# A hybrid decoder trunk on one core: the body inside a block that is ordered by the finer of the framework's two timelines

## The chip, the cores and the metric

One core of a Trainium2 chip runs the whole kernel. The metric is device time in microseconds (us) of one execution, as a median over runs. The engines are TensorE (PE, with its weight loader PEld), VectorE (DVE), ScalarE (ACT), GpSimd (POOL) and SyncE (SP), which here only issues transfers. Each engine works through its own queue in order; semaphores tie the queues together.

## The reference

Two layers, each on a stream x of 256 tokens by 1024 channels in float32. A layer normalises x and multiplies it by one wide matrix `w_in` (1024 by 12832). The result feeds three mixers side by side: a Mamba-2 scan (convolution, SiLU, chunked scan with decays), a sliding-window attention with sinks, and an attention with forgetting gates. Each has a SiLU gate and its own projection; the three are merged by sigmoid gates, pass one output projection and are added to x:

```python
for layer in range(DEPTH):
    h = rms_norm(x, norm_w[layer])
    proj = jnp.einsum('bsd,de->bse', h, w_in[layer])
    ...
    y_a = mamba2_branch(...)
    y_b = sliding_window_branch(...)
    y_c = forgetting_attention_branch(...)
    branch = jnp.einsum('bsiw,iwd->bsid', ys, w_proj[layer])
    g = jax.nn.sigmoid(gates.reshape(b, s, N_BRANCH, d) + gate_bias[layer])
    x = x + jnp.einsum('bsd,de->bse', jnp.sum(g * branch, axis=2), w_out[layer])
return rms_norm(x, final_norm_w)
```

## The kernel before, in words

**Precision and pieces.** Every wide product is taken in three passes of a rounded 32-bit type: both factors are split into a high and a low part, and high x high, low x high and high x low are added in PSUM. Weights come in pieces: SP loads a part of 1024 values per partition into one of six `raw` buffers, ScalarE copies it to `hi` (L290) and VectorE subtracts to get `lo` (L291); `hi` and `lo` have six buffers each, and at most four split parts are held ahead of their use (`AHEAD`, in `feed`). TensorE's products are all issued by the helpers `mm` (L109) and `transpose` (L113), so these two lines stand for all of its work.

**The order of TensorE** is written out: a list of operations (`ops`) is walked by `run_op`, and a small planner (`launch`, `pump`, `drain`) slips the short steps of attention and scan between the wide products at due times given by constants such as `D_SOFT` or `D_Q`, counted on an estimate of TensorE's time. These constants say how many microseconds lie between, say, the scores of an attention and the transposes of its probabilities; in that time ScalarE and VectorE must have done the softmax (L610 to L658; the scaling of the windowed one is L639).

**The order of the other engines** is the framework's. It traces all instructions, and when the trace is closed it walks through them on a timing model: whenever an engine of the model is free, it takes the instruction of highest priority (the earliest written, unless raised by `tc.high_priority`) whose inputs the model has ready. Buffers of a pool are given out in the same walk. The order that comes out is then fixed in each engine's queue; on the chip nothing is reordered. The kernel holds this choice by several means: `tc.manual_schedule` keeps the listed engines as written, `pin` (`keep_in_program_order`, L285) ties one instruction behind the one written before it on its engine, and `issue_after` (in `finish`) queues a group behind a given one.

```python
with tc.manual_schedule(engines={ENG.PE, ENG.DVE, ENG.Activation, ENG.Pool}):   # L1425
    ...
with tc.manual_schedule(engines={ENG.PE}):                                      # L1555
    for g in late:
        g()
    for i, f, last in ops[3:]:
        run_op(i, f, last)
```

The first region is the first stage of some 18 us: there the four compute engines are as written, and from then on TensorE alone.

**Lines that the prediction names.** `dma_sum` (L481 to L490) evicts two halves of a product with ScalarE (L486, L487) and lets GpSimd issue a transfer that adds one to the other (L488). The rotated queries and keys are multiplied by VectorE (L551) and combined by GpSimd (L561, L562). L676 ends the transposed probabilities of the windowed attention, L1106 adds a gate's bias while it frees TensorE's bank. L985 is a power on GpSimd with its VectorE reader L989 in `group_norms`; L257 and L259 are the same pair in `row_rsqrt2` at the end of a layer. In `mT` the merged branches are transposed and split again (pinned where marked, so its line is L285). L1205 to L1231 are the end of a layer's output: add, squares, root, scaling, store.

## Time and profile before

| | |
|---|---|
| runs | 806.71, 806.82, 807.55 us (median 806.82) |
| span of the profiled execution | 805.1 us |
| the rest of the median outside that span | 1.7 us |
| instructions in the span | 14840 |
| mean granted TensorE clock | 0.998 |

The span runs from the first to the last instruction of the profiled execution. Its rows give, for each engine, the busy time; for a group of instructions, their number, the mean of one and the idle time of the engine ahead of them with who ended it; and for a wait, how long in all, how many times and the longest. Matmuls overlap in their pipeline, so their mean duration is longer than the distance from one to the next. Idle time of an engine costs something only where TensorE then waits for it.

### The profile page before, as it was taken

The page shows a single profiled execution, that of the slowest core. Times are in us where ns is not written, and L with a number is a line of the kernel's source. Part 1 is how long each engine was busy: PE and PEld are TensorE (multiplying, and loading weights), DVE is VectorE, ACT ScalarE, POOL GpSimd, SP SyncE. Part 2 cuts the span into 40 slices and gives each one's busy share as a digit, 9 for nine tenths or more (in the row PEclk, how much of TensorE's full clock was granted, in tenths as well). Part 3 has the DMA queues.
Part 4 walks back from the last instruction along what each step waited for, and adds up shares of the span by engine and source line. Part 5 has one row for each costly group of instructions (what it writes and reads, how often), then busy time and mean ns, then how long its engine had stood idle before and what let it go on. Part 6 is the DMA issues. An engine that isn't in the chain of part 4 may idle for free.

```text
span 805.1 us, 14840 instructions
## 1 busy us (share of the span) xinstructions
PE 796.5 (99%) x5160; PEld 711.6 (88%) x5160; DVE 684.2 (85%) x1416; ACT 533.8 (66%) x1146; POOL 167.5 (21%) x236
## 2 busy tenths in 40 slices
PE   9999999999999999999999999999999999999996
PEld 8998988888998988888998899888889989888896
DVE  6878999997998997795785799999889999969865
ACT  7776768875775885543665678687657768755452
POOL 3166213140210100033001741122311220002000
PEclk9999999999999999999999999999999999999999
DMA  9997987797765565686678987679976546576632
GB/s 316 280 259 172 253 219 200 219 290 220 198 184 167 174 187 170 219 253 205 217 251 257 239 210 217 157 217 287 285 211 196 183 143 202 156 248 210 209 106 78
DMA packets 138827, 170.43 MB, mean 212 GB/s; under 512 B 9353, under 2 KB 106465, under 8 KB 138753
## 3 DMA queue, kind: packets, MB, share of 16 engines
q1 hardware_dynamic: 114960, 140.53, 55.5%
q0 software_dynamic: 13328, 13.29, 10.3%
q10 hardware_dynamic: 10464, 15.67, 6.7%
q8 instruction: 41, 0.67, 0.3%
q14 instruction: 34, 0.27, 0.1%
HBM read 154.71 MB, written 2.16 MB: 195 GB/s over the span
## 4 chain that ended last, share of the span: by engine, by line
PE 91%; issue 3%; DMA 2%; POOL 2%; DVE 1%; ACT 1%; POOLq 0%; DVEq 0%
PE mm L109 78%; PE mx L109 9%; PE mx L113 4%; DMA L<-L 1%; DMA hb<-in_sinks_dram 1%; POOL L L488 1%; DMA L<-in_x_dram 0%; DVE L L551 0%; ACT pp L610 0%; POOL L L285 0%; POOL L L562 0%; DVE lo L291 0%; POOL sm L224 0%; POOL L L571 0%; POOL L L572 0%
## 5 line engine op out<-in xcount | busy, mean ns | idle before, releaser
L109 PE MATMUL mm<-L,hi 128*128 128x512 f32 x1056 | 354.7, 387 | 0.5 <-ACT L L487 0.3
L291 DVE TENSOR_TENSOR lo<-raw,hi 128x1024 fp32r<-128x1024 f32 (+1 forms) x276 | 313.3, 1154 | 40.9 <-ACT hi L290 36.1
L109 PE MATMUL mm<-hi,L 128*128 128x512 f32 (+2 forms) x1168 | 303.1, 349 | 0.1
L290 ACT ACTIVATE hi<-raw 128x1024 fp32r<-128x1024 f32 (+1 forms) x276 | 265.6, 982 | 50.6 <-PE mm L109 30.0
L109 PE MATMUL mm<-L,lo 128*128 128x256 f32 x1056 | 266.6, 273 | 0.0
L109 PEld LDWEIGHTS mm<-hi,L 128*128 128x128 f32 x1168 | 205.8, 190 | 23.2 <-issue 1.5
L109 PEld LDWEIGHTS mm<-L,hi 128*128 128x128 f32 x1056 | 195.1, 190 | 27.4 <-issue 3.0
L109 PEld LDWEIGHTS mm<-L,lo 128*128 128x128 f32 x1056 | 202.1, 191 | 5.3
L109 PE MATMUL mm<-lo,L 128*128 128x512 f32 (+2 forms) x584 | 201.5, 347 | 0.0
L109 PEld LDWEIGHTS mm<-lo,L 128*128 128x128 f32 x584 | 110.2, 190 | 10.7
L488 POOL DMA_DIRECT2D L<-L x68 | 60.7, 915 | 192.5 <-ACT L L487 155.2
L1074 POOL TENSOR_SCALAR_AFFINE_SELECT bias<-bias 128x128 f32<-128x128 f32 x64 | 30.8, 513 | 82.7 <-DMA bias<-cumd 82.7
L829 DVE SCALAR_TENSOR_TENSOR L<-L,vec,L 128x255 f32<-128x255 f32 (+2 forms) x96 | 46.2, 481 | 1.9 <-ACT L L826 0.4
L486 ACT ACTIVATE L<-mm 128x256 f32<-128x256 f32 x84 | 31.9, 380 | 20.0 <-PE mm L109 14.0
L652 ACT ACTIVATE pp<-pp,nm 128x128 f32<-128x128 f32 x64 | 28.2, 443 | 22.8 <-DVE nm L646 22.8
L1109 ACT ACTIVATE L<-L 128x512 f32<-128x512 f32 x24 | 15.1, 631 | 34.5 <-DVE L L1106 30.8
L610 ACT ACTIVATE pp<-pp,nm 128x128 f32<-128x128 f32 x32 | 12.6, 394 | 24.9 <-DVE nm L615 24.1
L488 POOL DMA_DIRECT2D qt<-L x16 | 14.2, 925 | 71.4 <-ACT qt L487 64.6
L1142 POOL TENSOR_TENSOR L<-L,L 128x512 f32<-128x512 f32 x8 | 12.0, 1494 | 74.0 <-DVE L L1141 74.0
L487 ACT ACTIVATE L<-mm 128x256 f32<-128x256 f32 x68 | 26.2, 386 | 1.5 <-DMA L<-L 1.5
L1106 DVE TENSOR_TENSOR L<-mm,L 128x512 f32<-128x512 f32 x22 | 15.1, 687 | 11.2 <-PE mm L109 11.2
L551 DVE TENSOR_TENSOR L<-L,cs 128x256 f32<-128x256 f32 x40 | 20.0, 536 | 4.6 <-DMA L<-L 4.6
(213 smaller groups left out, 913.7 us busy)
## 6 DMA issues: line engine op xcount, KB each, us to landing
raw<-in_w_in_dram SPq DMA_DIRECT2D x191, 512.0 KB, 5.1
raw<-in_w_proj_dram SPq DMA_DIRECT2D x48, 512.0 KB, 6.0
L<-L POOLq DMA_DIRECT2D x72, 128.0 KB, 5.4
raw<-in_w_out_dram SPq DMA_DIRECT2D x16, 512.0 KB, 5.9
bias<-cumd ACTq DMA_DIRECT2D x16, 256.0 KB, 3.4
L<-cumd ACTq DMA_DIRECT2D x8, 512.0 KB, 5.4
L<-in_gate_bias_dram ACTq DMA_DIRECT2D x12, 256.0 KB, 5.4
qt<-L POOLq DMA_DIRECT2D x16, 128.0 KB, 6.0
```

What stands on the lines that cost most here:

```text
L109: nc.tensor.matmul(o, a, b, **kw)
L113: nc.tensor.transpose(o, a, i)
L290: keep(act)(hi, src, AF.Copy)
L291: keep(tt)(lo, src, hi.bitcast(F32), op=ALU.subtract)
L486: act(halves(lo), ordered(p[:, S:2 * S]), AF.Copy)
L487: last = act(halves(out), ordered(p[:, 0:S]), AF.Copy)
L488: nc.gpsimd.dma_start(out, lo, accum_op=ALU.add)
L551: tt(m, p, cs[:, i, :], op=ALU.mult)
L652: act(pp[:, i, sl], pp[:, i, sl], AF.Exp, scale=-1.0, bias=nm[:, e:e + 1], accum_out=sums[:, e:e + 1])
L829: stt(a[:, s:S], x_[:, 0:S - s], y.vec[:, 16 * j + u:16 * j + u + 1], a[:, s:S], op0=ALU.mult, op1=ALU.add)
L1074: nc.gpsimd.affine_select(out=bias[:, i, dst], in_=bias[:, i, src], compare_op=ALU.is_ge, fill=NEG, base=0, pattern=[[-1, P]], channel_mul ...
L1106: tt(halves(g), p, halves(y.gb), op=ALU.add)
```

## The change

One line is added in `hybrid_trunk`, ahead of the first instruction of the body; the pools are opened before it:

```diff
+    ctx.enter_context(tc.block(schedule_with_timeline_sim=True))
     nw8 = T("L1", [NK, P])
     nc.scalar.dma_start(nw8, norm_w[0:1, :].rearrange("o (k p) -> (o k) p", p=P))
     tab = T("tab", [P, 1])
```

`tc.block` traces what follows into a block of its own that is ordered as a unit: what is traced outside it is not mixed in. With the argument, the walk over the block's instructions runs on the finer of the framework's two timing models; without it, and in the kernel before, it runs on the coarser one. By the framework's own words the coarser one leaves out a fixed cost of GpSimd's elementwise instructions. No operation, tile, buffer count, pin or written order differs.

## The prediction

> **What bounds the kernel now.** I read the page's first lines, then a table of busy time by stage, then the list of who waits for whom on each engine, then the timeline at the places where TensorE starts just after its input. In the group rows below the number after the bar is the busy sum, then the mean of one in ns, then the idle time just before it and who ended it.

> ```profile
> span 805.1 us, 14840 instructions
> ...
> PE 796.5 (99%) x5160; PEld 711.6 (88%) x5160; DVE 684.2 (85%) x1416; ACT 533.8 (66%) x1146; POOL 167.5 (21%) x236
> ...
> L109 PEld LDWEIGHTS mm<-hi,L 128*128 128x128 f32 x1168 | 205.8, 190 | 23.2 <-issue 1.5
> L109 PEld LDWEIGHTS mm<-L,hi 128*128 128x128 f32 x1056 | 195.1, 190 | 27.4 <-issue 3.0
> ```

> The span is 805.1 us and the median of the runs 806.82, so 1.7 us lie outside the span; I add them to every sum. TensorE (PE) is busy 99% of it. A busy share can hide short gaps, so the next view matters more: the busy time of every engine in eight stages (start:end, length, then PE, weight loader, VectorE, ScalarE, GpSimd with their counts, granted clock, DMA share).

> ```profile
> 0.00:18.00 18.00, 16.20 (x112) 15.20 (x113) 12.27 (x27) 13.26 (x27) 5.40 (x20) 1.00 0.93 309
> 18.00:75.00 57.00, 56.87 (x377) 51.74 (x375) 45.29 (x80) 40.46 (x94) 26.37 (x35) 1.00 0.97 255
> 75.00:150.00 75.00, 74.78 (x559) 67.32 (x560) 72.34 (x189) 58.25 (x159) 18.71 (x24) 1.00 0.76 204
> 150.00:300.00 150.00, 149.87 (x1032) 133.38 (x1031) 137.76 (x320) 108.37 (x243) 25.37 (x42) 1.00 0.73 211
> 300.00:387.00 87.00, 87.00 (x435) 76.04 (x434) 65.50 (x80) 43.20 (x55) 16.78 (x18) 1.00 0.64 199
> 387.00:480.00 93.00, 93.00 (x596) 85.13 (x596) 70.92 (x124) 60.51 (x128) 29.00 (x35) 1.00 0.86 242
> 480.00:780.00 300.00, 299.93 (x1939) 265.63 (x1937) 264.48 (x566) 200.55 (x428) 45.87 (x64) 1.00 0.70 206
> 780.00:805.00 25.00, 18.83 (x122) 17.20 (x120) 15.67 (x36) 9.22 (x18) 0.00 (x0) 0.95 0.18 64
> ```

> Between 18 and 780 us PE is idle 0.13 + 0.22 + 0.13 + 0 + 0 + 0.07 = 0.55 us out of 762. The other idle time is 1.80 us ahead of 18 us and 6.17 us in the last stage, most of it after the last product. The granted clock is 1.00 wherever PE works steadily. So **TensorE's own stream is the whole time**: nothing that another engine does can shorten it by more than those crumbs. The list of PE's waits says the same; it has two entries (who waited for whom: total, times, longest):

> ```profile
> PE mx L113 <- POOL ident masks.py:199: 1.5, 1, 1.5
> PE mm L109 <- ACT L L487: 0.3, 1, 0.3
> ```

> The first is the identity matrix at the start, the second one eviction at 75 us.

> **The change part by part.** It adds one line: the body is traced inside a block that the framework orders by its finer timeline of the engines, where it used the coarser one before. No operation is added or removed: 5160 products, 1416 VectorE, 1146 ScalarE and 236 GpSimd instructions and every transfer stay. Three parts have to be priced.

> *TensorE's order* cannot move: from its first product to its last it stands in regions that keep it as written (L1425 and L1555). Price 0.

> *The first 18 us* (to the end of the first region) are written out by hand on the four compute engines, so only the SP queue's transfers could move there. They stand in one queue in program order, x and the first pieces of w_in ahead. Price 0; what could be won back there is at most the 1.80 us of PE idle of that stage.

> *The order on VectorE, ScalarE, GpSimd and of the transfers after that* is what moves. Each of these queues is in order, so an instruction that is put ahead of another delays everything behind it, and one that is put in front while its input is late holds its whole engine. Two things cover this. First, the weight pieces are split well ahead: ScalarE's split waits for PE to give a buffer back, and seldom the other way round.

> ```profile
> ACT hi L290 <- PE mm L109: 30.0, 43, 5.4
> ...
> DVE sm L989 <- POOL sm L985: 3.6, 2, 1.8
> DVE sm L259 <- POOL sm L257: 1.2, 2, 0.8
> ```

> ScalarE waits 43 times, 30.0 us in all, for buffers that PE still reads: the store of split pieces is full at those times, and one late split costs nothing. Second, the written order of PE leaves some microseconds between a step and its use. What a finer timeline could gain is in the other two rows: VectorE stands 3.6 + 1.2 = 4.8 us behind GpSimd's powers. That is VectorE's time, not PE's, so it is worth 0 here.

> The transfers move with their queues (in the rows: count, size, median us from issue to landing):

> ```profile
> raw<-in_w_in_dram SPq DMA_DIRECT2D x191, 512.0 KB, 5.1
> ...
> L<-L POOLq DMA_DIRECT2D x72, 128.0 KB, 5.4
> ```

> SP issues little but weight loads, one as each of six buffers comes free, so their order among themselves has no reason to change; GpSimd's adding transfers are issued behind ScalarE's evictions as now. I cost both at 0; the cover is the six buffers and the three evictions that stand between such a transfer and its reader. Without it one late transfer costs up to its 5.4 us, which is less than the upper bound below.

> The cover is thin at some places, and these carry my sum. In the timeline rows the first number is the start, the second the length; I pair the producer with PE's start behind it.

> ```profile
> 75.19 0.48 PE L109 MATMUL mm<-L,hi 128*128 128x512 f32 x1 [0.31 <-ACT L L487]
> ...
> 123.21 0.69 DVE L639 TENSOR_TENSOR pp<-pp,rsum 128x512 f32<-128x512 f32 x1
> ...
> 124.05 0.63 PE L113 MATMUL mx<-ident,pp 128*128 128x128 f32 x4
> ...
> 150.04 0.69 DVE L1106 TENSOR_TENSOR L<-mm,L 128x512 f32<-128x512 f32 x1
> ...
> 150.84 0.19 PEld L109 LDWEIGHTS mm<-L,hi 128*128 128x128 f32 x1 [0.40 <-issue]
> ...
> 159.78 0.69 DVE L676 TENSOR_TENSOR L<-mx,L 128x512 f32<-128x512 f32 x1
> ...
> 160.69 0.39 PE L109 MATMUL mm<-L,bias 128*64 128x256 f32 x2
> ...
> 386.06 0.69 DVE L285 SCALAR_TENSOR_TENSOR L<-mx,L 128x512 fp32r<-128x512 f32 x1 [0.90 <-ACT L L285]
> ...
> 386.80 0.19 PEld L109 LDWEIGHTS mm<-hi,L 128*128 128x128 f32 x1 [0.15 <-DVE L L285]
> ...
> 518.12 0.69 DVE L639 TENSOR_TENSOR pp<-pp,rsum 128x512 f32<-128x512 f32 x1
> ...
> 518.96 0.63 PE L113 MATMUL mx<-ident,pp 128*128 128x128 f32 x4
> ...
> 780.88 0.69 DVE L285 SCALAR_TENSOR_TENSOR L<-mx,L 128x512 fp32r<-128x512 f32 x1 [0.90 <-ACT L L285]
> ...
> 781.62 0.19 PEld L109 LDWEIGHTS mm<-hi,L 128*128 128x128 f32 x1 [0.16 <-DVE L L285]
> ```

> At 124.05 PE starts 0.15 us after the softmax scaling has ended (123.21 + 0.69 = 123.90); at 150.84 0.11 us after an add that frees its bank; at 160.69 0.22 us after a subtraction; at 386.80 and 781.62 0.05 us after a low half of `merged`. The second layer repeats the first 394.91 us later (518.96 - 124.05), so the middle three count twice: 3 x 2 + 75.19 + 386.80 + 781.62 makes **nine places** with at most 0.22 us to spare.

> The common filler that a new order can put ahead there is one split:

> ```profile
> L291 DVE TENSOR_TENSOR lo<-raw,hi 128x1024 fp32r<-128x1024 f32 x224 | 274.9, 1239 | 29.2 <-ACT hi L290 24.6 <-DMA raw<-in_w_proj_dram 1.6 <-PE mm L109 1.6
> ```

> It takes 1.24 us, so a place that gets one ahead costs 1.24 - 0.15 = 1.1 us. How many places are hit the trace cannot tell. Bounds: none (0) or all nine with two splits each, 9 x (2.48 - 0.15) = 21.0 us. I take five of nine with one split, 5.5 us: about half, because the rule of choice (highest priority among what is ready) stays and only the moments move, and because the two places on `merged` are partly pinned. Other steps have more room, and I cost them at nothing; their cover is the full store and PE's written distances. If that goes, the price is the fourth rival's.

> *The block's borders.* Everything but the pools lies inside, so no work can be cut off by it. The trace does not show such a border; the nearest rows are the entry into the body:

> ```profile
> 0.41 0.10 POOL L1581 MEMSET const-uint8-127<- 128x1 uint8 x1
> 0.81 0.20 POOL masks.py:197 MEMSET ident<- 128x128 f32 x1 [0.29 <-POOLq L1581]
> ```

> GpSimd passes from the preamble into the body in 0.4 us. Two borders: 0 to 0.8 us. I take 0.4. A gain I exclude, as a border only adds.

> Sum on the profiled execution: 805.1 + 5.5 + 0.4 = 811.0, and with 1.7 outside **812.7 us**.

> **The rivals.**

> *No difference (0.18).* The new order differs, but nowhere where PE has no room, or it differs little. For it: 0.55 us of PE idle in 762, and a full store of splits. Against it: nine places with at most 0.22 us. Time 805.2 to 808.4, most likely 807.2 with the borders. That the change does nothing at all (the pins and the written regions leave no freedom) belongs here too.

> *Faster (0.06).* The finer timeline frees VectorE of its waits for GpSimd and thereby the thin places. All that PE can win is 0.55 us in the middle and 1.80 in the first stage: 806.8 - 2.35 = 804.5. It decides only if more than 1.6 of these 2.35 us go; the 1.80 lie in the part written by hand, which speaks against it. The 6.17 us at the end are a chain that keeps its order:

> ```profile
> 798.56 0.28 PE L109 MATMUL mm<-lo,L 128*128 128x256 f32 x1
> 798.87 0.42 DVE L1205 TENSOR_TENSOR L<-mm,L 128x256 f32<-128x256 f32 x1 [0.26 <-PE mm L109]
> ...
> 801.45 0.36 SPq L1229 DMA_DIRECT2D out_dram<-L  x1
> ```

> From the last product at 798.56 to the issue of the output each step needs the one before.

> *Hidden room in PE (0.01, inside the chance of faster).* The weight loader is busy only 711.6 us. If its idle time were waits, an order that ended them all would give 711.6 + 1.8 + 6.2 + 1.7 = 721 us. Against it, the chain's row:

> ```profile
> 360.68 5.18 PE mm L109 x24
> ```

> 24 products of 512 columns in 5.18 us are 216 ns each, while a load takes 190 ns: the loader idles because the array streams. Only 1.5 + 3.0 = 4.5 us of its idle time are put down to something else. [...]

> *VectorE becomes the bound (0.10).* Between 75 and 150 us it is busy 72.34 of 75 us, so it has 2.66 us to lose. If the new order makes it wait for GpSimd or a transfer at the head of its queue more often, each microsecond beyond 2.66 reaches PE, in both layers. With one wait of 0.8 us (the longest one of the L259 row) for each of the 24 GpSimd instructions of the stage: 2 x (19.2 - 2.7) = 33 us, or 840 us. It decides from four waits per layer on, and I place it above 828.

> **How the numbers follow.** The forecast, slower by thin places, has 0.65; no difference 0.18; VectorE as the bound 0.10; faster 0.06 (with the 0.01); 0.01 is left for something else that costs time. A measurement of this kernel tells about 0.2% (1.6 us) from no change, so the borders are 805.2 and 808.4. Slower is 0.65 + 0.10 + 0.01 = 0.76. The forecast's own range is 808.4 to 828.2 (806.8 + 21.0 + 0.4). The range that should hold 8 in 10 takes in no difference and the best case, 804.5, and ends at 828; above it lies the 0.10 of VectorE.

> **What would show it.** Right: PE's instruction count and mean durations as before, PE idle between 18 and 780 us grown from 0.55 to about 6 us, and the list of PE's waits with some five to nine entries of about 1 us each, ended by VectorE (L639, L676, L1106, L285) or ScalarE (L487). The first 18 us and the end after the last product stay within 0.5 us. The splits (L291) stand at other places among the short instructions. Wrong: a list of PE's waits as short as now (no difference); PE waits of many microseconds between 75 and 150 us with VectorE waiting for GpSimd (the bound has moved); a gap at the start or the end (the block's borders cost what I put at 0.4); or a span below 803.5, which would need PE's stream itself to be shorter.

## The result and the profile after

The changed kernel takes **832.58 us** (median of 831.0 to 836.51), the kernel before 806.91 on the same chip: ratio 1.0325, 95% interval 1.0311 to 1.0338, or 25.7 us slower. The forecast was 812.7 with a range up to 828.0: the sign is right, the size is not. The profiled execution is the longest of the five, 836.51 us. From L182 on each line of the kernel after stands one number higher: L291 of before is L292 here.

The first lines of the page after:

```profile
span 834.8 us, 14888 instructions
...
PE 806.6 (97%) x5160; PEld 716.8 (86%) x5160; DVE 684.1 (82%) x1416; ACT 535.8 (64%) x1146; POOL 163.0 (20%) x236
```

There are as many products as before, but PE is busy 10.1 us longer (806.6 - 796.5), and 48 instructions have come in, all of them waits on semaphores. The table by stage of the kernel after (start:end, length, then busy time of PE, weight loader, VectorE, ScalarE and GpSimd with their counts, granted clock, DMA share):

```profile
0.00:18.00 18.00, 15.21 (x107) 13.61 (x108) 11.82 (x27) 12.80 (x25) 4.78 (x19) 1.00 0.91 302
18.00:75.00 57.00, 57.00 (x381) 52.17 (x380) 45.08 (x85) 42.55 (x101) 25.31 (x35) 1.00 0.95 257
75.00:150.00 75.00, 69.91 (x518) 62.20 (x517) 66.04 (x176) 52.94 (x146) 21.04 (x24) 0.98 0.76 201
150.00:300.00 150.00, 149.08 (x997) 133.15 (x996) 134.55 (x307) 106.64 (x237) 22.23 (x42) 1.00 0.72 205
300.00:387.00 87.00, 85.59 (x444) 73.55 (x443) 68.94 (x91) 47.00 (x65) 16.91 (x18) 1.00 0.63 199
387.00:480.00 93.00, 91.18 (x567) 82.45 (x566) 62.13 (x100) 51.05 (x96) 22.07 (x28) 0.98 0.79 226
480.00:780.00 300.00, 290.13 (x1883) 256.17 (x1883) 260.34 (x576) 199.75 (x449) 49.40 (x70) 0.99 0.69 198
780.00:835.00 55.00, 48.47 (x278) 43.55 (x276) 35.19 (x58) 23.05 (x34) 1.28 (x1) 0.96 0.37 120
```

Between 18 and 780 us PE is now idle 5.09 + 0.92 + 1.41 + 1.82 + 9.87 = 19.1 us, where it was 0.55. The first stage lost 1.0 us and the next one made it good: set beside the same product of before, PE is 0.6 us late at 18 us and 0.1 at 75. After that it is 7.7 us late at 150, 9.0 at 300, 10.9 at 387, 14.7 at 480 and 29.6 at the end. So the loss begins in the stage from 75 to 150 us and comes back in the second layer. The list of PE's waits after (who for whom: total, times, longest):

```profile
PE mx L113 <- DVE sums L637: 3.9, 2, 2.0
PE mx L109 <- DVE L L797: 3.8, 2, 1.9
PE mx L109 <- DVE L L961: 2.5, 2, 1.2
PE mm L109 <- DVE L L1107: 2.4, 1, 2.4
PE mm L109 <- DVE L L480: 2.2, 4, 0.9
PE mm L109 <- DVE L L292: 1.8, 1, 1.8
...
PE mm L109 <- ACT L L488: 1.3, 2, 0.6
PE mx L109 <- ACT hi L1465: 0.9, 2, 0.6
PE mm L109 <- DVE L L677: 0.6, 2, 0.3
```

Nearly all entries come in pairs, once in each layer. The two largest are the end of the window softmax (101.59 us) and the small sums of decays of the scan (124.11 us); neither is among the nine thin places. In the timeline of before these two places look so (the first row is two scalings of 0.69 us each, of which PE's transposes need the first; PE's row stands below its input):

```profile
98.40 1.29 DVE L639 TENSOR_TENSOR pp<-pp,rsum 128x512 f32<-128x512 f32 x2
99.49 0.60 PE L113 MATMUL mx<-ident,pp 128*128 128x128 f32 x4
...
115.93 0.19 DVE L796 TENSOR_TENSOR L<-dt,nega 128x32 f32<-128x32 f32 x1
117.94 0.38 PE L109 MATMUL mx<-tri,L 128*128 128x128 f32 x2
```

**Two costs for one wait.** The granted clock of 0.98 in the third stage is new. The same table in windows of 3.41 us, after:

```profile
121.14:124.55 3.41, 1.50 (x11) 1.18 (x10) 3.31 (x17) 0.29 (x1) 0.00 (x0) 1.00 1.12 294
124.55:127.97 3.42, 3.42 (x15) 3.06 (x14) 3.36 (x21) 3.03 (x16) 0.00 (x0) 0.50 0.06 12
...
97.25:100.66 3.41, 2.40 (x21) 2.20 (x19) 3.24 (x20) 2.76 (x14) 0.00 (x0) 1.00 0.09 30
100.66:104.08 3.42, 1.85 (x12) 1.56 (x13) 3.17 (x7) 3.42 (x11) 0.98 (x2) 1.00 0.00 0
104.08:107.49 3.41, 3.41 (x23) 3.16 (x22) 3.40 (x4) 3.41 (x8) 0.20 (x1) 1.00 0.89 228
```

In the window from 121.14 PE is busy 1.50 us, and the whole next one runs at a clock of 0.50: about 1.7 us lost. The equally long wait at 101.59 lies across two windows, which keep 2.40 and 1.85 us of work, and the clock stays. There are four such stretches of 3.41 us in the work of the profiled execution (from 124.55, 418.10, 534.15 and 571.70 us), which lose 4 x 1.7 = 6.8 us together; before there was none until the last product. Idle time up by 28.2 - 8.6 = 19.6 us and busy time up by 10.1 are the 29.7 us of span. Set beside the same products of before, the last product is 29.6 us late: 22.6 of these arise at products that waited, 6.8 in the half-clock stretches, and 0.3 elsewhere. So the waits and the clock are the whole loss; the waits cost some 3 us more than PE's idle time says, probably because the product ahead of a wait counts as busy to its modelled end.

**Where VectorE loses its time.** Who waits for whom on VectorE in this stage, first of the kernel before (75 to 152 us), then of the one after (72 to 160 us):

```profile
DVE lo L291 <- ACT hi L290: 0.7, 1, 0.7
DVE L L836 <- ACT L L835: 0.5, 1, 0.5
DVE sums L636 <- ACT es L635: 0.2, 1, 0.2
```

```profile
DVE L L944 <- ACT L L943: 4.6, 3, 3.1
DVE lo L292 <- ACT hi L291: 3.2, 6, 1.0
DVE sums L637 <- ACT es L636: 1.5, 3, 0.5
DVE L L837 <- ACT L L836: 1.1, 2, 0.5
```

It was 1.4 us and is 10.4. VectorE had 2.66 us to lose here (72.34 busy of 75), so what goes beyond that can reach PE. The largest part of it, 3.1 us, is one event. GpSimd's rows around 78 us, before and after (start, length, operation):

```profile
77.84 0.86 POOL L561 TENSOR_TENSOR qt<-L,L 128x256 f32<-128x256 f32 x1 [1.53 <-DVE L L551]
78.65 0.84 POOL L488 DMA_DIRECT2D L<-L  x1
```

```profile
77.79 2.96 POOL L562 TENSOR_TENSOR qt<-L,L 128x256 f32<-128x256 f32 x1 [1.56 <-DVE L L552]
80.70 0.86 POOL L489 DMA_DIRECT2D L<-L  x1
```

The same product starts at the same time and takes 2.96 us in place of 0.86. Behind it in GpSimd's queue stands the issue of an adding transfer (`dma_sum`), now 2.05 us later. ScalarE and VectorE after:

```profile
86.08 0.42 ACT L943 ACTIVATE L<-L 128x256 f32<-128x256 f32 x1 [3.49 <-DMA L<-L]
```

```profile
77.96 0.72 DVE L292 TENSOR_TENSOR lo<-raw,hi 128x544 fp32r<-128x544 f32 x1
78.60 0.42 DVE L944 SCALAR_TENSOR_TENSOR L<-L,L 128x256 f32<-128x256 f32 x1
78.94 1.22 DVE L292 TENSOR_TENSOR lo<-raw,hi 128x1024 fp32r<-128x1024 f32 x1
...
86.53 0.43 DVE L944 SCALAR_TENSOR_TENSOR L<-L,L 128x256 f32<-128x256 f32 x1 [3.11 <-ACT L L943]
```

ScalarE's L943 heads its queue and waits 3.49 us for that transfer, VectorE's L944 waits behind it for 3.11, and behind it VectorE runs some 3.3 us later than before, up to the first instruction of the window softmax (L616 at 96.60, before 93.29). The second layer repeats the event (L562 at 486.85 takes 2.96 us again). While GpSimd's product lasts, VectorE runs from one instruction to the next without a pause (77.96 to 80.15); the product ends 0.6 us after the last of them. Before, the split behind the pair of products was the one that took longer, 1.55 us for 816 columns where the same split takes 1.00 elsewhere:

```profile
78.01 1.55 DVE L291 TENSOR_TENSOR lo<-raw,hi 128x816 fp32r<-128x816 f32 x1
```

So at this place one of the two engines takes longer in either kernel: GpSimd after (2.96 against 0.86 us), VectorE before (1.55 against 1.00). Why, the traces do not show.

### The profile page after: what moved, and what is told of

Its sections match the earlier page's. It is cut to its first block, busy times and chain, and to the rows that moved or that the text cites. A ratio compares the mean times of both kernels' runs of the same rounds, so it can differ in the third digit from the quotient of the medians.

```text
span 834.8 us, 14888 instructions
## 1 busy us (share of the span) xinstructions
PE 806.6 (97%) x5160; PEld 716.8 (86%) x5160; DVE 684.1 (82%) x1416; ACT 535.8 (64%) x1146; POOL 163.0 (20%) x236
## 3 DMA queue, kind: packets, MB, share of 16 engines
q10 hardware_dynamic: 10464, 15.67, 5.9%
## 4 chain that ended last, share of the span: by engine, by line
PE 74%; DVE 12%; issue 5%; ACT 4%; DMA 4%; POOL 1%; ACTq 0%; SPq 0%; DVEq 0%; POOLq 0%
PE mm L109 65%; PE mx L109 7%; DVE lo L292 4%; PE mx L113 2%; DMA L<-L 2%; ACT hi L291 1%; DVE L L830 1%; DMA L<-in_x_dram 1%; DMA raw<-in_w_in_dram 1%; DVE L L295 0%; DVE mx L624 0%; DVE pp L616 0%; DVE L L480 0%; ACT pp L611 0%; DVE nm L625 0%
## 5 line engine op out<-in xcount | busy, mean ns | idle before, releaser
L109 PE MATMUL mm<-L,hi 128*128 128x512 f32 x1056 | 358.9, 390 | 6.1 <-DVE L L1107 2.4
L292 DVE TENSOR_TENSOR lo<-raw,hi 128x1024 fp32r<-128x1024 f32 (+1 forms) x276 | 311.2, 1147 | 47.0 <-ACT hi L291 43.6
L109 PE MATMUL mm<-hi,L 128*128 128x512 f32 (+2 forms) x1168 | 304.4, 350 | 2.3 <-DVE L L292 1.8
L291 ACT ACTIVATE hi<-raw 128x1024 fp32r<-128x1024 f32 (+1 forms) x276 | 265.8, 983 | 56.6 <-PE mm L109 40.8
L109 PE MATMUL mm<-L,lo 128*128 128x256 f32 x1056 | 268.6, 275 | 0.0
L109 PEld LDWEIGHTS mm<-hi,L 128*128 128x128 f32 x1168 | 206.7, 190 | 26.1 <-DVE L L292 2.1
L109 PEld LDWEIGHTS mm<-L,hi 128*128 128x128 f32 x1056 | 197.4, 191 | 34.8 <-issue 5.6
L109 PEld LDWEIGHTS mm<-L,lo 128*128 128x128 f32 x1056 | 204.0, 193 | 5.3
L109 PE MATMUL mm<-lo,L 128*128 128x512 f32 (+2 forms) x584 | 202.1, 348 | 0.0
L109 PEld LDWEIGHTS mm<-lo,L 128*128 128x128 f32 x584 | 110.5, 190 | 10.8
L1075 POOL TENSOR_SCALAR_AFFINE_SELECT bias<-bias 128x128 f32<-128x128 f32 x64 | 24.7, 420 | 103.3 <-DMA bias<-cumd 103.3
L487 ACT ACTIVATE L<-mm 128x256 f32<-128x256 f32 x84 | 32.2, 384 | 18.0 <-PE mm L109 14.7
L653 ACT ACTIVATE pp<-pp,nm 128x128 f32<-128x128 f32 x64 | 28.2, 442 | 22.5 <-DVE nm L647 22.5
L943 ACT ACTIVATE L<-L 128x256 f32<-128x256 f32 x48 | 19.9, 415 | 16.3 <-DMA L<-L 10.6
L1107 DVE TENSOR_TENSOR L<-mm,L 128x512 f32<-128x512 f32 x22 | 15.1, 687 | 16.8 <-PE mm L109 9.6
L944 DVE SCALAR_TENSOR_TENSOR L<-L,L 128x256 f32<-128x256 f32 x48 | 19.9, 422 | 10.9 <-ACT L L943 10.8
L113 PE MATMUL mx<-ident,pp 128*128 128x128 f32 x160 | 23.1, 276 | 3.9 <-DVE sums L637 3.9
## 6 DMA issues: line engine op xcount, KB each, us to landing
raw<-in_w_in_dram SPq DMA_DIRECT2D x191, 512.0 KB, 5.0
raw<-in_w_proj_dram SPq DMA_DIRECT2D x48, 512.0 KB, 5.8
L<-L POOLq DMA_DIRECT2D x72, 128.0 KB, 5.5
raw<-in_w_out_dram SPq DMA_DIRECT2D x16, 512.0 KB, 5.5
L<-cumd ACTq DMA_DIRECT2D x8, 512.0 KB, 6.0
qt<-L POOLq DMA_DIRECT2D x16, 128.0 KB, 5.5
```

What stands on the lines that cost most here:

```text
L109: nc.tensor.matmul(o, a, b, **kw)
L113: nc.tensor.transpose(o, a, i)
L291: keep(act)(hi, src, AF.Copy)
L292: keep(tt)(lo, src, hi.bitcast(F32), op=ALU.subtract)
L487: act(halves(lo), ordered(p[:, S:2 * S]), AF.Copy)
L653: act(pp[:, i, sl], pp[:, i, sl], AF.Exp, scale=-1.0, bias=nm[:, e:e + 1], accum_out=sums[:, e:e + 1])
```

## The experiments

Most kernels hold engines to an order by a chain of order-only links. It is laid over the instructions of an engine, in the order that a build of before or after gave them, at the end of the body:

```diff
+def _hold(tc, engine, order):
+    found = [i for i in tc.nc.cur_bb.bb.instructions
+             if i.engine == engine and type(i).__name__ != "InstRegisterMove"]
+    for a, b in zip(order, order[1:]):
+        tc.add_manual_dep(found[b], found[a].name,
+                          mybir.DependencyInfo(mybir.DependencyClass.NoSync, mybir.DependencyReason.DATA),
+                          reason="hold")
```

OLD and NEW below are an engine's order in the kernel before and in the changed one; in the kernels they stand as lists of numbers. The chains hold 1318 instructions of VectorE, 1064 of ScalarE and 232 of GpSimd (the profile's 1416 of VectorE count 98 readings of an accumulator apart). New VectorE with old ScalarE, or the reverse, has no run here: where one engine is held alone, the framework chooses the other's order anew.

### Block or order: e1_plain_block and f_all_new

```diff
-    ctx.enter_context(tc.block(schedule_with_timeline_sim=True))
+    ctx.enter_context(tc.block())
```

> The changed kernel with the block kept and only the option that lets the framework choose the order taken away. In the program every engine's instructions then stand in the order of the kernel before; only the block's borders remain. Theory (the order costs the 25.7 us): 806.5 to 807.8 us, within the spread of the kernel before, with the products idle 0.6 us between 18 and 780 us and no stretch at a granted clock of 0.50. Rival (the block itself, its border and its added semaphore instructions, costs the time): about 832 us, or a part of the 25.7 us that stays with the borders.

Measured: 806.82 us, ratio 1.0000 (0.9991 to 1.0010). The block and its borders cost nothing that can be measured. PE's waits come to 2.0 us in its trace, where they were 1.8 before (1.5 of them for the identity matrix in both), and no half-clock stretch stands in its work.

The counterpart is the kernel before with the three orders and no block:

```diff
+    _hold(tc, ENG.DVE, NEW_DVE)
+    _hold(tc, ENG.Activation, NEW_ACT)
+    _hold(tc, ENG.Pool, NEW_POOL)
```

> The kernel before, without any block, with VectorE, ScalarE and GpSimd held to the orders of the changed kernel; TensorE and SyncE stand as before. Theory (the orders of these three engines are the whole loss): 831 to 834 us. Rival (the block, TensorE's two moved products at 15 us or SyncE's one moved load take part): below by their share, at most 1 us for the start.

Measured: 831.23 us, ratio 1.0305 (1.0288 to 1.0322). The orders of these three engines are the loss; whether TensorE's two products, SyncE's one load and the block add anything to it is below what the intervals can tell.

### One engine: e2_dve_old, e3_act_old, e4_dve_new

```diff
+    _hold(tc, ENG.DVE, OLD_DVE)
```

> The changed kernel with VectorE alone held to the order of the kernel before by 1415 order-only links; the framework still chooses for ScalarE (121 instructions stand elsewhere than before) and GpSimd (18). Theory (VectorE's order makes the late evictions): 807 to 813 us, TensorE idle under 6 us between 18 and 780 us, and neither the 1.9 us wait at the window softmax (ended by L637) nor the one at the decay sums (ended by L797). Rival (ScalarE's and GpSimd's order makes them): 825 to 832 us, both waits still there.

```diff
+    _hold(tc, ENG.Activation, OLD_ACT)
```

> The changed kernel with ScalarE alone (and the transfers it starts) held to the order of the kernel before; VectorE stays free (238 instructions stand elsewhere than before). Theory (VectorE's order makes the loss): 825 to 835 us, with the waits ended by L637 and L797 at about 1.9 us each in both layers and two or more stretches of 3.4 us at a granted clock of 0.50. Rival (ScalarE's order makes it): 807 to 813 us.

```diff
+    _hold(tc, ENG.DVE, NEW_DVE)
```

> The kernel before, without any block, with VectorE alone held to the order that it has in the changed kernel (277 instructions moved); ScalarE adapts (144 moved), GpSimd hardly (6), TensorE and the transfers of SyncE stand as before. Theory (VectorE's order alone makes the loss): 825 to 835 us, with the waits at the window softmax and at the decay sums as in the changed kernel. Rival (it takes ScalarE's order, GpSimd's or the block as well): 807 to 813 us. In between: the loss is made by VectorE and ScalarE together, and the waits that appear say which belong to VectorE.

The first two are edits of the changed kernel, the third one of the kernel before. Measured: 818.73 us (ratio 1.0142, 1.0125 to 1.0159), 828.17 (1.0264, 1.0249 to 1.0279) and **863.69** (1.0704, 1.0678 to 1.0729). The theory that VectorE's order alone carries the loss fell: e2_dve_old gives back 13.9 of the 25.7 us and stays above its bound of 813, and VectorE's new order beside one that the framework then chose for ScalarE is far worse than the changed kernel. Only the time of e3_act_old lies where this theory had it (825 to 835), with a wait at the softmax of 0.9 us and not 1.9. A row of each engine of e2_dve_old shows why:

```profile
100.56 1.23 DVE L292 TENSOR_TENSOR lo<-raw,hi 128x1024 fp32r<-128x1024 f32 x1 [1.95 <-ACT hi L291]
```

```profile
99.46 1.07 ACT L291 ACTIVATE hi<-raw 128x1024 fp32r<-128x1024 f32 x1
```

VectorE keeps the low half of a split between two steps of the softmax, as before. ScalarE, in the order that the framework chose for it here, has its high half behind all eight exponentials; before it stood between the fourth and the fifth. VectorE waits 1.95 us at the head of its queue and the softmax behind it is late by as much. So this loss lies in how two queues fit together.

### One place repaired: g1_site1, g3_decay_old, g4_both_old

All three are the changed kernel with all three engines held to the new order, and the old one put back in one or two stretches of each layer. g1_site1 takes 72 to 92 us, g3_decay_old 103 to 119 us, g4_both_old both. Written as a loop (the kernels have the finished lists):

```diff
+    order = list(NEW_DVE)
+    for p, q in stretches:
+        order[p:q] = OLD_DVE[p:q]
+    _hold(tc, ENG.DVE, order)
+    ...
```

> The changed kernel, every engine held to its order there except in one stretch of each layer, about 72 to 92 us after the start and its copy in the second layer: there VectorE (44 instructions a layer), ScalarE (40) and GpSimd (2) have the order of the kernel before. In the changed kernel GpSimd's product of the rotation (L562) takes 2.96 us in this stretch against 0.86 us before, the transfers that GpSimd issues behind it are late, ScalarE's L943 waits 3.49 us for one of them, VectorE stands idle 3.11 us behind that, and from there on VectorE runs 3.3 us late. Theory A (that lateness is what reaches TensorE at the window softmax, 98.7 us, and at the decay sums, 116.7 us): both waits shrink, 819 to 824 us. Theory B (the softmax is hit by it, the decay sums by their own order): 826 to 828 us. Rival C (the sites are late by their own order, not by this stretch): 831 to 834 us.

> The changed kernel, every engine held to its order there, except that around the decay sums of each layer (about 103 to 119 us) VectorE (43 instructions a layer) and ScalarE (30) have the order of the kernel before. Theory A (VectorE comes 3.3 us late into this stretch, and that is what makes the decay sums late): 829 to 833 us. Theory B (the chain of short instructions from L780 to L797 is cut apart by splits, taps and evictions in the new order): 824 to 826 us, the wait at the decay sums gone and that at the softmax left.

> The changed kernel with both stretches, 72 to 92 us and 103 to 119 us of each layer, in the order of the kernel before, the rest in the order of the changed one. Both theories: the waits at the softmax and at the decay sums go, with the half-clock stretches behind them: 832.6 - 2 x (3.0 + 3.8) = 819 us, 817 to 821 us. More than 824 us would say that a third stretch feeds these waits.

Measured: 826.54 us (ratio 1.0245, 1.0228 to 1.0262), 835.45 (1.0358, 1.0339 to 1.0377) and 828.48 (1.0267, 1.0250 to 1.0283). In g1_site1 GpSimd's product takes 0.86 us again, the wait at the softmax is gone and the one at the decay sums stays: theory B of that run. But repairing the decay sums made the kernel no faster, against both theories, and repairing both is not better than repairing the first alone. The PE waits of g3_decay_old:

```profile
PE mm L109 <- DVE L L1107: 6.2, 2, 3.1
PE mx L113 <- DVE sums L637: 4.0, 3, 2.0
```

The waits for L797 have gone, and now PE waits 3.1 us in each layer for L1107, the gate bias, where in the changed kernel it waited 2.4 us once. I read it so: a wait of PE inside this stage gives VectorE time, and if it is taken away, VectorE is as late at the next place, since its lost time is still lost. What counts is then the sum over the stage: VectorE is idle between the same first and last instruction of 75 to 151 us for 2.7 us before, 11.6 after, 8.6 in g1_site1, 12.1 in g3_decay_old and 8.1 in g4_both_old. The times follow this order, except that g4_both_old comes out 1.9 us above g1_site1; its profiled execution has two half-clock stretches, that of g1_site1 one.

### The same places put into the kernel before: g2_site1_new_min, g5_decay_new

```diff
-VectorE: 291 628 636 551 638 634 551 639 636 638 639 | 551 551 291 | 291
+VectorE: 636 628 638 634 639 636 638 639 291 551 551 | 291 551 551 | 291
```

The diff has the lines of the first layer's instructions; g2_site1_new_min changes the part ahead of the first bar (11 instructions, and 11 in the second layer; one pair of products and one split are among them, fewer than its expectation says). g5_decay_new has 103 to 119 us in the new order on VectorE and ScalarE.

> The kernel before, all engines held to its order, except for 11 VectorE instructions of each layer at about 75 to 81 us (the last sums of the window softmax, two pairs of the rotation's products and three splits), which stand in the order of the changed kernel. Theory A: these 11 suffice to keep GpSimd's product (L561) from its operands for 2.5 us or more, and VectorE loses about 3 us behind it: 811 to 814 us if only the softmax is hit, up to 819 us if the decay sums are too. Rival (the stretch needs ScalarE's and GpSimd's new order as well, or does no harm by itself): 806.5 to 808 us.

> The kernel before, all engines held to its order, except that around the decay sums of each layer (103 to 119 us) VectorE (43 instructions a layer) and ScalarE (30) have the order of the changed kernel. Theory A (the decay sums are late in the changed kernel only because VectorE arrives 3.3 us late): 806.5 to 809 us. Theory B (the new order of the decay chain is late by itself): the wait at the decay sums appears in both layers, 810 to 815 us.

Measured: 808.82 us (ratio 1.0029, 1.0013 to 1.0045) and 809.72 (1.0039, 1.0024 to 1.0054). In the profiled execution of g2_site1_new_min the 11 instructions do not do it: GpSimd's product took 0.86 us. That execution took 807.85 us, though, and the ten runs spread from 806.77 to 812.44, some of the long ones at an unchanged clock (810.53 at 0.999); whether GpSimd's product takes longer in those is not known. In g5_decay_new the new order of the decay chain is late by itself: PE waits 1.8 us for L796 in each layer (theory B, just under its bound), and 2.9 of these 3.6 us stay in the time.

### Three instructions: i1_three_old, i2_three_new

Between the bars stand three instructions: the last pair of the rotation's products and one split. i1_three_old is the changed kernel with these three in the old order, 6 instructions of 1318:

```diff
-VectorE: 292(816 columns) 552 552 292(816) 552 552 292(544)
+VectorE: 292(816 columns) 552 552 552 552 292(816) 292(544)
```

i2_three_new is the kernel before with the 11 and these three in the new order.

> The changed kernel, every engine held to its order there, except for three VectorE instructions of each layer at about 76 us: the last two of the rotation's products (L552) stand ahead of the 816-column split (L292) as in the kernel before, and not behind it with the 544-column split next. Theory (what VectorE does right behind the pair decides whether GpSimd's product gets at its operands): L562 takes 0.9 us and not 2.96, L943 waits under 1 us, the wait at the window softmax falls from 1.9 us to under 0.7, and the time is near that of the repair of the whole stretch, 826 us (824 to 829). Rival (it takes the whole stretch): 831 to 835 us.

> The kernel before, every engine held to its order, except for 14 VectorE instructions of each layer at about 75 to 81 us in the order of the changed kernel: the 11 of the earlier run (808.8 us) and the three around the last two products of the rotation. Theory: GpSimd's product takes 2.5 us or more, VectorE loses some 3 us behind it and TensorE waits 1 to 2 us at the window softmax in both layers: 810 to 815 us. Rival: 807 to 809.5 us as with the 11.

Measured: **826.59 us** (ratio 1.0246, 1.0230 to 1.0261), as much as the whole stretch gave back, and 819.06 (1.0153, 1.0138 to 1.0168), 10 us above the run without the three and 4 above its bound. GpSimd's product in i1_three_old, then in i2_three_new, and VectorE's longest wait there:

```profile
76.09 0.85 POOL L562 TENSOR_TENSOR qt<-L,L 128x256 f32<-128x256 f32 x1 [0.64 <-DVE L L552]
```

```profile
78.76 4.44 POOL L561 TENSOR_TENSOR qt<-L,L 128x256 f32<-128x256 f32 x1 [3.68 <-DVE L L551]
```

```profile
DVE L L943 <- ACT L L942: 7.1, 1, 7.1
```

So in these four profiled executions (with the changed kernel and g2_site1_new_min) the place of one split decides whether GpSimd's product takes 0.9 us or 3.0 to 4.4. Not settled is why: in both GpSimd starts 0.16 us into VectorE's last product, and the width of the split behind it does not decide, since in e3_act_old a 544-column split follows as well and GpSimd's product took 0.85 us (the split 1.28).

### The stage and the rest: i3_stage_old, i4_stage_new

The whole stage from 72 to 158 us of each layer on all three engines: old in the changed kernel, then new in the kernel before, by the same edit as in g1_site1 with wider bounds.

> The changed kernel, every engine held to its order there, except in the whole stage from 72 to 158 us of each layer, where VectorE (202 instructions a layer), ScalarE (161) and GpSimd (25) have the order of the kernel before. Theory (VectorE's lost time in this stage makes most of the loss, two smaller places behind it the rest): the waits at the group norms (L961, about 1.2 us each layer, with 0.9 us ahead of it) and at the layer border (L292, 1.8 us) remain, 813 to 817 us. Rival (the stage's loss moves to a later place, as it did in the repairs of single places): above 820 us.

> The kernel before, every engine held to its order, except in the whole stage from 72 to 158 us of each layer, which has the order of the changed kernel on VectorE, ScalarE and GpSimd. Theory: the stage's loss alone, 806.9 + 15 to 20 = 822 to 827 us, with VectorE's waits in the stage at about 10 us a layer against 1.4. Rival (the order of the whole program works together): under 815 us.

Measured: 815.96 us (ratio 1.0117, 1.0101 to 1.0134) and 825.11 (1.0227, 1.0212 to 1.0242). 18.4 us are the stage's and 9.3 the rest's (measured against 806.68), 27.7 together for the 25.7 of the whole. The rest is what the PE waits of i3_stage_old show; 8.5 of the 9.0 us by which its last product is late arise at products that waited:

```profile
PE mx L109 <- DVE L L961: 2.5, 2, 1.2
PE mm L109 <- DVE L L480: 2.3, 4, 1.0
...
PE mm L109 <- DVE L L292: 1.3, 1, 1.3
```

These are the squares for the group norms, evictions ahead of them, and one split at the border of the layers.

### Which wait costs clock: h1_gaps

```diff
         r = nc.tensor.matmul(o, a, b, **kw)
+        if gap["last"] is not None:
+            tc.add_manual_dep(r.ins, gap["last"].ins.name, gap["info"], reason="gap")
+            gap["last"] = None
+        elif gap["plan"] and clock["t"] >= gap["plan"][0][0]:
+            n = gap["plan"].pop(0)[1]
+            g = [nc.gpsimd.memset(scr, 0.0) for _ in range(n)]
+            tc.add_manual_dep(g[0].ins, r.ins.name, gap["info"], reason="gap")
+            gap["last"] = g[-1]
```

> The kernel before, VectorE and ScalarE held to its order, with 36 artificial waits of TensorE between 170 and 730 us: after one product GpSimd clears a scratch tile 6, 10, 13, 16, 20 or 26 times (six waits of each size, in mixed order, about 16 us apart), and the next product waits for it. The time itself says little; the trace gives the length of each wait and the granted clock behind it. Theory (a wait of about 2 us or more can drop the granted clock to 0.50 for 3.4 us, one of 1 us doesn't): no half-clock stretch behind the shortest waits, one behind most of those over 2 us, each costing about 1.7 us. Rival (the half clock in the changed kernel has another trigger): no relation to the length of the wait.

Measured: 1013.83 us, with 36 waits of 1.4 to 7.1 us, longer than meant. It is not the length alone that decides: a wait of 3.45 us (364.91 to 368.36) left the clock, one of 2.65 (496.31 to 498.96) did not. All half-clock stretches in the work of this trace start at whole multiples of 3.413 us from one another, and last one, two or three times as long. On that grid (PE's busy time, then the granted clock):

```profile
192.75:196.17 3.42, 1.33 (x6) 1.20 (x7) 1.40 (x2) 0.00 (x0) 1.51 (x10) 1.00 0.99 273
196.17:199.58 3.41, 3.41 (x10) 2.66 (x9) 0.00 (x0) 0.00 (x0) 0.00 (x0) 0.50 0.56 190
387.31:390.72 3.41, 1.61 (x8) 1.08 (x6) 3.41 (x4) 2.41 (x4) 1.21 (x9) 1.00 0.68 206
390.72:394.13 3.41, 1.75 (x8) 1.56 (x9) 0.61 (x2) 0.00 (x0) 1.21 (x8) 1.00 0.91 314
```

A window with 2.08 us idle is followed by half clock. A wait of 3.46 us split into 1.80 and 1.66 between two windows is not. Laid over the 11 traces with such stretches in their work, and counting windows at full clock ahead of the last product: after 43 of 43 windows with 1.99 us idle or more the clock fell, after 10 of 16 with 1.82 to 1.96, after none of 60 with 1.00 to 1.81. So the theory holds with one amendment: the idle time counts by window, and what a wait costs depends on where it falls. The runs of the changed kernel spread over 5.5 us, three stretches of 1.7. Their mean granted clocks go the same way at the ends, 0.990 in the longest run and 0.997 in the shortest, but do not order the three between (0.994, 0.993, 0.993 from the longer to the shorter); as only one run was profiled, this reason is argued and not shown.

No experiment points to an order that beats the kernel before: the best of them only returns to it.

## Why the prediction was wrong

- *TensorE's stream is the whole time; nothing can be won there.* Right. No kernel came out under 806.8.
- *TensorE's order cannot move: price 0.* The statement was wrong, the price right: two products stand four products earlier, at 14.2 us and not 14.7. PE was 0.6 us late at 18 us and 0.1 at 75.
- *The block's borders: 0.4 us.* Measured 0 (e1_plain_block).
- *A new order costs where PE has nothing to spare.* The kind of loss is right (f_all_new), and the waits of PE are ended by VectorE and ScalarE as foreseen.
- *Five of nine thin places at 1.1 us each.* **This is the step that failed**: it took the places one by one and let one misplaced split of 1.24 us be the largest harm. Of the nine, the trace after shows a loss at one, the second layer's copy of the place at 150.84 (L1107, 2.4 us); that is 2.4 of some 20 us of new waits. The waits for L677 belong to an earlier use of that line, at 112.29 and 507.20 us of the kernel before. What the runs show in its place is time that VectorE loses over the whole stage, 11.6 us idle where it was 2.7, and a stage worth 18.4 us (i4_stage_new) where the forecast had 5.5 for the whole kernel.
- *Other steps have more room, and I cost them at nothing.* This let the rest through. The largest waits are at the end of the window softmax and at the decay sums. In the kernel before VectorE was done 0.4 us ahead of PE at the one (98.40 + 0.69 = 99.09, PE at 99.49) and 1.8 at the other (115.93 + 0.19 = 116.12, PE at 117.94). That is more than the thin places have, but VectorE came 3.3 us late into the softmax and was still 2.4 late with its first scaling (101.45), which leaves 2.0 us beyond the 0.4; PE waited 1.9.
- *GpSimd's adding transfers and their order: cost 0; without the cover up to 5.4 us.* The uncovered case came: the transfer issued at 80.70 us reached L943 at 86.08, after 5.4 us, and put VectorE 3.1 us behind. Taking away what delayed it gave back 6.0 us (i1_three_old).
- *VectorE becomes the bound (0.10).* This rival had the mechanism: 2.66 us to lose between 75 and 150 us, waits at the head of a queue, each microsecond beyond that reaching PE in both layers. Its price was off the other way: 10.4 us of waits in the stage and not 19.2, all ended by ScalarE (the longest by a transfer behind it) and not by GpSimd. The stage's measured share, 18.4 us (i4_stage_new), lies between the forecast and this rival's 33. With the waits of that run's trace, 9.9 us in the first layer, the rival's own sum gives an estimate of 2 x (9.9 - 2.7) = 14.4 us, and the two half-clock stretches there add 3.4: 17.8 of the 18.4. It should have been the likeliest case, since its row was the only one of the stage table with under 4% to spare beside PE's.
- *What a wait costs.* I priced each at its length. Four half-clock windows made 6.8 us of the profiled execution's 29.7; no row of before could show them, as PE never stood still there.

## What to carry to other kernels

Where one engine is full and a second one has as little as 3 or 4% to spare in a stage, do not price a reordering by the places where the first one starts late; sum what the second one may lose over the stage, because a wait repaired at one place comes back at the next. Look first for what its queue can be held by: a partner engine whose order must match, and a transfer issued behind a slow GpSimd instruction. And where TensorE runs without a gap, the first waits of about 2 us may cost nearly twice their length, as at the decay sums here: 1.9 us of wait and 1.7 us lost to the half clock behind it, in both layers.

## What the hardware did that I had not expected

**A product of GpSimd lasted several times as long beside VectorE.** That of 128x256 took 0.85 us in i1_three_old, 2.96 in the changed kernel while three VectorE instructions ran back to back, and 4.44 and 5.68 behind five and seven (first layer of i2_three_new and e4_dve_new). In these last three cases it ended 0.6 us after the last of the row, and not at the next border between two instructions.
